# A residual kept in DRAM as one tensor per slice, with the short sequence's feed-forward layers gathering into it, and a new order of seven products

## The chip, the core and the metric

The kernel runs on one core of a Trainium2 chip. The metric is the device time of one execution in microseconds; three executions of the kernel before are known, and one more was recorded by the hardware profiler.

## What is computed

One encoder layer is applied to two sequences that share all weights: a short one, P (512 tokens), and a long one, S (1024 tokens), with 1024 channels each. All of it is fp32.

```
x = x + 1/2 * g1 * SwiGLU1(mod(RMSNorm(x)))
u = mod(RMSNorm(x)); [q|k|v|hv|hx1|hx2] = u @ w_in
a = 2-D neighbourhood attention(q, k, v)
h = bidirectional order-2 Hyena(hv, hx1, hx2)
x = x + g2 * (concat(RMSNorm(a), RMSNorm(h)) @ w_out)
x = x + 1/2 * g3 * SwiGLU2(mod(RMSNorm(x)))
...
def swiglu(x, w_gate, w_up, w_down):
    return (jax.nn.silu(x @ w_gate) * (x @ w_up)) @ w_down
```

The shifts, scales and gains (sh, sc, g1 to g3) come from a small product with `w_ada`. The hidden width of the two feed-forward layers (FFN) is 2816, that is 22 blocks of 128.

## The kernel before

**Layout.** Activations are held transposed: 128 channels on the partitions, 512 tokens along a row. A sequence's residual x is `q.xT[c]`, where c is a chunk of 512 tokens (P has one chunk, S two), and has KT = 8 slices of 128x512 in it. An fp32 product is made of three matmuls of halves (a high part and a low part of each factor), so the matmul that counts is one of 128x512, which starts about every 0.23 us when nothing stands in its way.

**The FFNs.** The 22 blocks are taken two at a time, in 11 groups g. In each group the gate and up products are formed (tiles `gu`, and `mx` in S), SiLU and product follow on ScalarE and VectorE (tiles `s`, `a`, `act`), and the down product goes slice by slice (dt = 0 to 7) into one of two PSUM banks `dn`, six matmuls each. What becomes of `dn` differs. For P (`ffn`) the residual lies in SBUF, and VectorE adds gain times `dn` to it in one instruction (`stt`, seen as `xTp<-dn` or `xRp<-dn`). For S (`ffn_fast`) the residual lies in DRAM (`q.xscr`): ScalarE writes gain times `dn` into one of four small tiles (two `s`, two `a`), and GpSimd issues a DMA that adds the tile to DRAM (line 805). Only the last group of S reads the residual back and ends as P does. S's gate and up products take seven products where eight would be usual, over sums of blocks (Strassen's way); `PRODUCTS` is the order of the seven, A and S being blocks of weights, B and T blocks of activations. B11 and B21 come from chunk 0 alone, and every T needs both chunks.

**Stages.** P's chain is narrow and S's work fills it up. `merge` takes steps of a main generator and of a side one, and the numbers in `PLAN` (cost of the main work, cost of the side work, lead of the side work, fraction) say how far the side is to be at each point of the main one. In stage A the main work is P's first FFN, and beside it stand the hyena filters of both sequences and the products with `w_ada` (DMAs into `wada6a` and `wada6b`). In stage D the main work is P's output projection and second FFN, and beside it stands S's hyena and attention. S's own FFNs run alone. By the trace stage A lies from 34 to 592 us, S's first FFN from 794 to 1487, the P projection of D from 1864 to 1930, S's hyena from 1930 to 2230, S's attention from 2230 to 2442, the tail of D to 2496, S's output projection to 2597 and S's second FFN to 3271.

**Queues.** Each engine works its instructions in program order. Weights are loaded by SyncE's queue (line 152). GpSimd issues all other DMAs (`dmb`, line 155, and the gathers, line 805) one after the other, and a DMA whose data is not there yet stops those behind it. Line 130 is the matmul; lines 116 and 118 are the instructions of VectorE and ScalarE, 118 for those of a side generator.

Of the kernel before, what the change touches and what calls it, by code (L numbers as in the profile page):

```python
# [17 lines left out]
P = 128  # L18
# [74 lines left out]
def build(ctx, tc, nc, A):  # L93
# [107 lines left out]
    for qn, L in SEQ_LEN.items():  # L201
# [20 lines left out]
        q.xscr = dp.tile([q.C, P, KT * 512], F32, name=f"xscr_{qn}")  # L222
# [285 lines left out]
    def spill_x(q):  # L508
        for c in range(q.C):
            for i in range(0, KT, 2):  # L510
                dmb(q.xscr[c][:, i * 512:(i + 2) * 512], q.xT[c][:, i:i + 2].rearrange("p k t -> p (k t)"))

    def reload_x(q, c, b):
        if c == 0:
            q.xT = []
        q.xT.append(blk(b, [P, KT, 512], F32, f"xR{q.n}"))
        dmb(q.xT[c].rearrange("p k t -> p (k t)"), q.xscr[c])


    def ffn(q, hn, wg, wu, wd, k, after, gate=None, last=None, get_dn=None,  # L520
            begin=None):
# [5 lines left out]
        def down(g, cs_, acts):  # L527
            wds = [load_unit(wd[(g * F + f) * P:(g * F + f + 1) * P, :], ()) for f in range(F)]
            for c in cs_:
                sq = SumSq()  # L530
                for dt in range(KT):
                    ps = (get_dn or dn)()
                    for f in range(F):
                        wh, wl = (wds[f][dt // 4][:, i, (dt % 4) * P:(dt % 4 + 1) * P] for i in range(2))
                        act = acts[f, c]
                        mm(ps, wh, act[:, 0:512], f == 0, False)
                        mm(ps, wh, act[:, 512:1024], False, False)
                        mm(ps, wl, act[:, 0:512], False, f == F - 1)
                    xv = q.xT[c][:, dt]
                    stt(xv, ps, q.Gc[:, k, dt:dt + 1], xv, ALU.mult, ALU.add)  # L540
                    if g == NG - 1:
                        if last is not None:
                            last.add(c, dt)
                        else:
                            sq.add(xv)
                    if dt == 3 and q.C == 1:
                        yield
                if g == NG - 1:
                    if last is not None:
                        last.done(c)  # L550
                    else:
                        after(c, sq)
                yield
        late = None
        for n, (g, cs_) in enumerate(passes):
            acts = {}
            for f in range(F):
# [33 lines left out]
                if late is not None and (f == F - 1 or n < len(passes) - 1):  # L591
                    yield from late
                    late = None
            late = down(g, cs_, acts)
# [11 lines left out]
    PRODUCTS = (("A11", "B11"), ("S1", "T1"), ("S2", "T2"), ("A12", "B21"), ("S3", "T3"), ("S4", "B22"),  # L606
# [63 lines left out]
    class Pair:  # L670
# [33 lines left out]
        def product(self, n, T):  # L704
# [3 lines left out]
            to, start = ((0, True), (2, True), (0, False), (1, True), (0, False), (2, False), (0, False))[n]  # L708
# [9 lines left out]
            elif n == 1:  # L718
                se.copy(k[3], b[2])
            elif n == 2:  # L720
                se.copy(k[1], b[0])
            elif n == 3:
                tt(k[0], k[0], b[1], ALU.add)
# [6 lines left out]
    def ffn_fast(q, fast, wg, wu, wd, k, after, last, scratch, xblocks):  # L730
# [4 lines left out]
        for g in range(NG):  # L735
# [12 lines left out]
            for n, (_, b) in enumerate(PRODUCTS):  # L748
# [3 lines left out]
                if end and n < 2:  # L752
                    if n == 0:
                        q.xT = []
                    reload_x(q, n, xblocks[n])
# [28 lines left out]
            for c in (1, 0):  # L784
                sq = SumSq()
                for dt in range(KT):
# [7 lines left out]
                    gain = q.Gc[:, k, dt:dt + 1]  # L794
                    if end:
                        xv = q.xT[c][:, dt]
                        stt(xv, ps, gain, xv, ALU.mult, ALU.add)
# [4 lines left out]
                    else:  # L802
                        y = (t_s, t_a)[dt % 2]()
                        se.activation(y, ps, AF.Copy, scale=gain)
                        nc.gpsimd.dma_start(q.xscr[c][:, dt * 512:(dt + 1) * 512], y, accum_op=ALU.add)  # L805
# [683 lines left out]
    for kt in range(KT):  # L1489
        tt(xr[kt], Pq.xT[0][:, kt], rs0, ALU.mult)  # L1490
    next(cols, None)
# [30 lines left out]
    def p_front():  # L1522
# [5 lines left out]
        yield from ffn(Pq, hn1, A["ffn1_w_gate"], A["ffn1_w_up"], A["ffn1_w_down"], 0, after, gate1, begin=begin1)  # L1528
# [15 lines left out]
    def s_input():  # L1544
# [4 lines left out]
        for c in range(2):  # L1549
# [14 lines left out]
            for kt in range(KT):  # L1564
                dmb(S.xscr[c][:, kt * 512:(kt + 1) * 512], z[c][kt])
            rows.append(rstd_rows(rstd_cols(ss, D), mx))
            yield
        fast.append(Fast(S, 0, z, rows, {"B11": 0, "T1": 5, "T2": 4, "B21": 1, "T3": 2, "B22": 3, "T4": 6}))
        for nm in ("B11", "T1", "T2", "B21"):
# [9 lines left out]
    def after1(c, sq):  # L1579
        hn2[c] = hn_pair(*((2, 3), (4, 1))[c], "hn2")  # L1580
        norm_mod(S, 1, hn2, c, sq)
    run(ffn_fast(S, fast[0], A["ffn1_w_gate"], A["ffn1_w_up"], A["ffn1_w_down"], 0, after1, None, 7, (0, 5)))
# [21 lines left out]
    def p_mixer():  # L1604
# [10 lines left out]
        w = blk(5, [P, 4096], F32, "hyP")  # L1615
# [6 lines left out]
        reload_x(Pq, 0, 5)  # L1622
# [6 lines left out]
    def after2(c, sq):  # L1629
        hn3p.append(hn_pair(2, 3, "hn3p"))  # L1630
        norm_mod(Pq, 2, hn3p, 0, sq)

    def p_back():
        yield from out_proj(Pq, mxP[0], 0, after2)
        yield from ffn(Pq, hn3p, A["ffn2_w_gate"], A["ffn2_w_up"], A["ffn2_w_down"], 2, None, None,
# [5 lines left out]
    def s_mixer():  # L1641
        fm = blk(4, [P, 4096], F32, "hyF")
        at = blk(1, [P, 4096], F32, "hyA")
# [7 lines left out]
        kT = [blk(i, [P, 4, 1024], F32R, "kTs") for i in (4, 1)]  # L1651
# [12 lines left out]
        mxS.append(hn_pair(4, 1, "mxs"))  # L1664
# [9 lines left out]
    def after3(c, sq):  # L1674
        rows3.append(rstd_of(sq.done(), D))
        z3.append([S.xT[c][:, kt] for kt in range(KT)])
        for i in range(0, KT, 2):
            dmb(S.xscr[c][:, i * 512:(i + 2) * 512], S.xT[c][:, i:i + 2].rearrange("p k t -> p (k t)"))
        if c == 0:
            fast.append(Fast(S, 2, z3, rows3, {"B11": 0, "T1": 1, "T2": 4, "B21": 6, "T3": 2, "B22": 3, "T4": 5}))  # L1680
# [8 lines left out]
    reload_x(S, 1, 5)  # L1689
# [4 lines left out]
    def any_ps():  # L1694
# [3 lines left out]
                 Final(S, any_ps, lambda c, b: t_act()), 7, (0, 1)))  # L1698
# [3 lines left out]
PLAN = {"A": (726e3, 509e3, 0.0, 0.94), "C": (321e3, 176e3, 0.0, 0.94), "D": (586e3, 413e3, 0.0, 0.94)}  # L1702
# [41 lines left out]
```

## Time and profile before

| | |
|---|---|
| median of 3 executions | 3304.14 us (3303.08 to 3305.0) |
| profiled execution, its own time | 3315.62 us |
| span of the profiled execution | 3313.8 us |
| TensorE busy (PE) | 3116.6 us, 94% |
| VectorE (DVE) | 2012.5 us, 61% |
| ScalarE (ACT) | 1440.1 us, 43% |
| GpSimd (POOL) | 548.7 us, 17% |

The time is the span and 1.8 us around it. The profiled execution took 11.5 us (0.35%) more than the median. PE is TensorE's matmuls and PEld its weight loads, which overlap them; a busy share is an average over stages that have different limits. Where busy time is shown by stretch, the columns are the stretch, its length, the busy time (and number of instructions) of PE, PEld, DVE, ACT and POOL, the granted clock of TensorE, the busy share of the 16 DMA engines, and GB/s. A row of waits gives the waiting engine, tile and line, what it waited for, the total in us, the number of times and the longest.

### The profile page before, as it was taken

What the parts mean: (1) busy time and instruction counts of PE and PEld (TensorE: products, weight loads), DVE (VectorE), ACT (ScalarE), POOL (GpSimd) and SP (SyncE); (2) the same over time, 40 slices, a digit from 0 to 9 for tenths busy, and PEclk for the clock granted to TensorE, in tenths of its full rate; (3) what the DMA queues carried; (4) which work ended last, traced back from release to release, by engine and by line L of the source; (5) the groups of instructions that cost most, each with busy time, mean ns of one, the idle gap of its engine ahead of it and who ended that gap; (6) DMA issues with size and microseconds to landing.
All of it is one profiled execution on the core that took longest, in us unless ns stands there. A gap on an engine that the chain in (4) does not pass through costs nothing. (4 is left out here: it accounts for less than half of the span.)

```text
span 3313.8 us, 41364 instructions
## 1 busy us (share of the span) xinstructions
PE 3116.6 (94%) x15283; PEld 2512.2 (76%) x15283; DVE 2012.5 (61%) x3720; ACT 1440.1 (43%) x2606; POOL 548.7 (17%) x809
## 2 busy tenths in 40 slices
PE   6989998989999999999999999989989899999998
PEld 4876777777777777777788878867768677777877
DVE  4763588768434434455676589986677734434435
ACT  3221223346444444544533332226664554544545
POOL 1121000220221221122211100002300021121120
PEclk8999999999999999999999999999989999999999
DMA  7458534464675575575335533344535375575573
GB/s 247 115 152 301 183 101 130 128 199 144 110 126 115 108 129 113 112 187 167 123 115 166 168 126 122 115 142 122 141 106 154 89 130 111 112 126 112 114 127 121
DMA packets 317690, 456.44 MB, mean 138 GB/s; under 512 B 19616, under 2 KB 224568, under 8 KB 310864
## 3 DMA queue, kind: packets, MB, share of 16 engines
q0 software_dynamic: 83600, 227.28, 30.6%
q1 hardware_dynamic: 233856, 226.52, 22.6%
q8 instruction: 120, 1.97, 0.3%
q14 instruction: 82, 0.67, 0.1%
q10 hardware_dynamic: 32, 0.01, 0.0%
HBM read 310.33 MB, written 152.78 MB: 140 GB/s over the span
## 5 line engine op out<-in xcount | busy, mean ns | idle before, releaser
L130 PE MATMUL dn<-act,hl 128*128 128x512 f32 x3168 | 775.9, 398 | 37.1 <-ACT a L116 16.2
L130 PEld LDWEIGHTS dn<-act,hl 128*128 128x128 f32 x3168 | 584.6, 189 | 209.0 <-ACT a L116 35.9
L116 DVE TENSOR_TENSOR hl<-raw,hl 128x512 fp32r<-128x512 f32 x606 | 412.5, 688 | 361.8 <-ACT hl L116 359.2
L116 ACT ACTIVATE hl<-raw 128x512 fp32r<-128x512 f32 x606 | 379.2, 630 | 563.5 <-PE gu L130 272.5
L116 DVE TENSOR_TENSOR hl<-mscA,hl 128x512 fp32r<-128x512 f32 x132 | 90.8, 689 | 342.3 <-ACT hl L116 341.1
L805 POOL DMA_DIRECT2D xscr_s<-s x160 | 136.8, 855 | 872.8 <-ACT s L116 866.3
L130 PE MATMUL gu<-hn3ph,hl 128*128 128x512 f32 x704 | 227.4, 401 | 12.0 <-DVE hl L116 9.8
L130 PE MATMUL gu<-T,hl 128*128 128x512 f32 x924 | 225.3, 391 | 5.1 <-ACT T L116 2.8
L130 PE MATMUL gu<-hn1ph,hl 128*128 128x512 f32 x704 | 226.4, 401 | 0.5 <-DVE hl L116 0.5
L130 PE MATMUL mx<-T,hl 128*128 128x512 f32 x924 | 224.2, 390 | 0.0
L130 PE MATMUL gu<-hn2h,hl 128*128 128x512 f32 x640 | 207.8, 402 | 1.8 <-DVE hl L116 1.5
L130 PEld LDWEIGHTS gu<-T,hl 128*128 128x128 f32 x924 | 172.8, 188 | 43.6 <-ACT T L116 4.3
L130 PEld LDWEIGHTS mx<-T,hl 128*128 128x128 f32 x924 | 173.3, 188 | 36.6 <-ACT act L116 0.4
L130 PEld LDWEIGHTS gu<-hn3ph,hl 128*128 128x128 f32 x704 | 134.4, 192 | 43.6 <-DVE hl L116 10.2
L130 PEld LDWEIGHTS gu<-hn1ph,hl 128*128 128x128 f32 x704 | 134.3, 193 | 40.1 <-issue 5.4
L130 PE MATMUL gu<-B,hl 128*128 128x512 f32 x660 | 160.7, 391 | 1.2 <-DVE hl L116 1.2
L130 PE MATMUL mx<-B,hl 128*128 128x512 f32 x660 | 159.9, 391 | 1.8 <-ACT act L116 1.8
L116 ACT ACTIVATE s<-dn,Gc_s 128x512 f32<-128x512 f32 x160 | 109.9, 687 | 117.2 <-DMA xscr_s<-s 82.3
L116 ACT ACTIVATE a<-dn,Gc_s 128x512 f32<-128x512 f32 x160 | 110.1, 688 | 116.7 <-DMA xscr_s<-a 82.1
L805 POOL DMA_DIRECT2D xscr_s<-a x160 | 137.0, 856 | 112.6 <-ACT a L116 107.4
L130 PEld LDWEIGHTS mx<-B,hl 128*128 128x128 f32 x660 | 124.0, 188 | 28.3 <-ACT act L116 2.2
L130 PEld LDWEIGHTS gu<-B,hl 128*128 128x128 f32 x660 | 124.2, 188 | 27.5 <-DVE hl L116 1.7
(448 smaller groups left out, 5571.6 us busy)
## 6 DMA issues: line engine op xcount, KB each, us to landing
raw<-in_ffn_w_gate SPq DMA_DIRECT2D x88, 512.0 KB, 3.9
xscr_s<-s POOLq DMA_DIRECT2D x160, 256.0 KB, 5.5
xscr_s<-a POOLq DMA_DIRECT2D x160, 256.0 KB, 5.4
raw<-in_ffn_w_up SPq DMA_DIRECT2D x66, 512.0 KB, 4.0
raw<-in_w_in SPq DMA_DIRECT2D x48, 512.0 KB, 4.3
raw<-in_ffn_w_down SPq DMA_DIRECT2D x44, 512.0 KB, 3.6
mscA<-in_ffn_w_down SPq DMA_DIRECT2D x44, 512.0 KB, 3.6
wada6a<-in_w_ada SPq DMA_DIRECT2D x12, 1024.0 KB, 7.5
```

Of the source, the lines that this page charges most:

```text
L116: return fn(*a, **k)
L130: nc.tensor.matmul(out, lhsT, rhs, start=start, stop=stop, skip_group_check=resume)
L805: nc.gpsimd.dma_start(q.xscr[c][:, dt * 512:(dt + 1) * 512], y, accum_op=ALU.add)
```

## The change

It has four parts. First, `q.xscr`, one DRAM tensor of 128x4096 per chunk, becomes eight tensors of 128x512, so that a spill or a reload of a chunk is eight DMAs of 256 KB in place of four of 512 KB or one of 2 MB. Second, P's two FFNs do as S's do: for the first ten groups ScalarE scales and GpSimd gathers, through the new function `gather`; P's residual is spilled ahead of each FFN and read back, slice by slice, after the down product of group 9. Third, `PRODUCTS` has A12 B21 in second place, and the banks and copies of `product` follow. Fourth, numbers: blocks 1 and 5 change places in several stages, and in `PLAN` the costs of the main work of A and D fall by 53e3 and the side work of A gets a lead of 0.08.

```diff
-        q.xscr = dp.tile([q.C, P, KT * 512], F32, name=f"xscr_{qn}")
+        q.xscr = [[dp.tile([P, 512], F32, name=f"xscr{c}{k}_{qn}") for k in range(KT)] for c in range(q.C)]
...
-    def spill_x(q):
-        for c in range(q.C):
-            for i in range(0, KT, 2):
-                dmb(q.xscr[c][:, i * 512:(i + 2) * 512], q.xT[c][:, i:i + 2].rearrange("p k t -> p (k t)"))
+    def spill_x(q, cs=None):
+        for c in range(q.C) if cs is None else cs:
+            for k in range(KT):
+                dmb(q.xscr[c][k], q.xT[c][:, k])
...
         q.xT.append(blk(b, [P, KT, 512], F32, f"xR{q.n}"))
-        dmb(q.xT[c].rearrange("p k t -> p (k t)"), q.xscr[c])
...
+        for k in range(KT):
+            dmb(q.xT[c][:, k], q.xscr[c][k])
+
+    def gather(q, k, c, dt, ps):
+
+        y = (t_s, t_a)[dt % 2]()
+        se.activation(y, ps, AF.Copy, scale=q.Gc[:, k, dt:dt + 1])
+        nc.gpsimd.dma_start(q.xscr[c][dt], y, accum_op=ALU.add)
...
-                    xv = q.xT[c][:, dt]
-                    stt(xv, ps, q.Gc[:, k, dt:dt + 1], xv, ALU.mult, ALU.add)
                     if g == NG - 1:
+                        xv = q.xT[c][:, dt]
+                        stt(xv, ps, q.Gc[:, k, dt:dt + 1], xv, ALU.mult, ALU.add)
                         if last is not None:
                             last.add(c, dt)
                         else:
                             sq.add(xv)
+                    else:
+                        gather(q, k, c, dt, ps)
...
                     late = None
+                    if g == NG - 1:
+                        reload_x(q, 0, xblock)
...
-    PRODUCTS = (("A11", "B11"), ("S1", "T1"), ("S2", "T2"), ("A12", "B21"), ("S3", "T3"), ("S4", "B22"),
+    PRODUCTS = (("A11", "B11"), ("A12", "B21"), ("S1", "T1"), ("S2", "T2"), ("S3", "T3"), ("S4", "B22"),
                 ("A22", "T4"))
...
-                if end and n < 2:
-                    if n == 0:
-                        q.xT = []
-                    reload_x(q, n, xblocks[n])
+                if end and n in (0, 2):
+                    reload_x(q, n // 2, xblocks[n // 2])
...
-PLAN = {"A": (726e3, 509e3, 0.0, 0.94), "C": (321e3, 176e3, 0.0, 0.94), "D": (586e3, 413e3, 0.0, 0.94)}
+PLAN = {"A": (673e3, 509e3, 0.08, 0.94), "C": (321e3, 176e3, 0.0, 0.94), "D": (533e3, 413e3, 0.0, 0.94)}
```

Three places of the program show what moves. The first is VectorE in S's hyena, late in stage D; `hyA` and `hyz` are the hyena's tiles, `hl` the halves of P's weights, `xRp` P's residual. Before:

```order
L116 TENSOR_TENSOR hl<-raw,hl 128x512
L116 SCALAR_TENSOR_TENSOR xRp_14116<-dn,Gc_p,xRp_14116 128x512 x2
L116 TENSOR_TENSOR hl<-raw,hl 128x512
L118 TENSOR_TENSOR hyA_14153<-hyA_14153,mx 128x512
L116 TENSOR_TENSOR hl<-raw,hl 128x512
L118 TENSOR_TENSOR hyA_14153<-hyA_14153,mx 128x512 x3
L116 SCALAR_TENSOR_TENSOR xRp_14116<-dn,Gc_p,xRp_14116 128x512
L118 TENSOR_TENSOR hyA_14153<-hyA_14153 128x2x256
L116 SCALAR_TENSOR_TENSOR xRp_14116<-dn,Gc_p,xRp_14116 128x512
```

With the change, at the same point of the hyena:

```order
L116 TENSOR_TENSOR hl<-raw,hl 128x512
L118 TENSOR_TENSOR hyz6b<-mx,hyz6b 128x512 x2
L118 TENSOR_TENSOR hyA_14385<-hyA_14385,mx 128x512 x4
L118 TENSOR_TENSOR hyA_14385<-hyA_14385 128x2x128
L118 TENSOR_TENSOR hyA_14385<-hyA_14385 128x2x256
L116 TENSOR_TENSOR hl<-raw,hl 128x512
L118 TENSOR_TENSOR hyA_14385<-hyA_14385 128x2x256
```

The additions to P's residual are gone from VectorE's queue; nothing takes their place there.

The second is GpSimd in S's attention, where `atS<-gwin` are loads of the bias, `mscA<-qscr_s` and `mscA<-vwin_s` loads of queries and values. Before:

```order
L155 DMA atS_16600<-gwin 16x1024 x2
L155 DMA mscA<-qscr_s 128x2x128
L155 DMA atS_16600<-gwin 16x1024
L155 DMA mscA<-vwin_s 128x3x256
L155 DMA atS_16600<-gwin 16x1024
L155 DMA atS_16600<-gwin 64x1024
```

With the change:

```order
L155 DMA atS_16889<-gwin 16x1024 x2
L155 DMA mscA<-qscr_s 128x2x128
L155 DMA atS_16889<-gwin 16x1024
L155 DMA mscA<-vwin_s 128x3x256
L155 DMA atS_16889<-gwin 16x1024
L155 DMA atS_16889<-gwin 64x1024
L524 DMA xscr_p<-s 128x512
L524 DMA xscr_p<-a 128x512
L524 DMA xscr_p<-s 128x512
L524 DMA xscr_p<-a 128x512
L155 DMA mscA<-qscr_s 128x2x128 x2
L155 DMA mscA<-vwin_s 128x3x256
```

The gathers (line 524 of the changed kernel) stand between the loads of one step of the attention and those of the next.

The third is GpSimd at the end of stage D, after the attention's last load, up to the spill that follows S's output projection. Before, nothing of P is there:

```order
L155 DMA mscA<-vwin_s 128x3x256
L155 DMA xRs_18958<-xscr_s 128x4096
L155 DMA xRs_19337<-xscr_s 128x4096
L155 DMA xscr_s<-xRs_18958 128x1024 x4
L155 DMA xscr_s<-xRs_19337 128x1024 x4
```

With the change, the gathers of group 9 and the reloads of P's residual (`xRp<-xscr_p`) alternate:

```order
L155 DMA xRs_19390<-xscr_s 128x512 x8
L524 DMA xscr_p<-s 128x512 x2
L155 DMA xRp_19399<-xscr_p 128x512
L524 DMA xscr_p<-a 128x512 x2
L155 DMA xRp_19399<-xscr_p 128x512
L524 DMA xscr_p<-s 128x512
L155 DMA xRp_19399<-xscr_p 128x512
L524 DMA xscr_p<-a 128x512
L524 DMA xscr_p<-s 128x512
L155 DMA xRp_19399<-xscr_p 128x512
L524 DMA xscr_p<-a 128x512
L155 DMA xRp_19399<-xscr_p 128x512 x4
```

Eight gathers and eight reloads have come in; a reload waits for the landing of the gather of its slice, and the gathers behind it wait with it. The same stands at the end of stage A.

## Rows read from the trace of the kernel before

**Rows 1.** The page: span, and busy time of TensorE and of VectorE

```profile
span 3313.8 us, 41364 instructions
...
PE 3116.6 (94%) x15283; PEld 2512.2 (76%) x15283; DVE 2012.5 (61%) x3720; ACT 1440.1 (43%) x2606; POOL 548.7 (17%) x809
```

**Rows 2.** Busy time by stretch: A, hyena, attention, S's second FFN

```profile
34.00:592.00 558.00, 516.18 (x2725) 402.49 (x2724) 359.57 (x645) 144.05 (x252) 53.00 (x92) 0.96 0.52 165
...
1930.00:2230.00 300.00, 285.07 (x1452) 241.02 (x1452) 278.64 (x489) 85.59 (x140) 17.16 (x32) 0.97 0.40 123
2230.00:2442.00 212.00, 201.41 (x1196) 154.40 (x1196) 139.79 (x409) 134.04 (x300) 59.05 (x93) 0.98 0.46 137
...
2597.00:3271.00 674.00, 650.31 (x2793) 520.88 (x2794) 310.09 (x470) 333.53 (x547) 136.89 (x162) 1.00 0.61 117
```

**Rows 3.** Waits of TensorE, 1930 to 2230: total, times, longest (us)

```profile
PE gu L130 <- DVE hl L116: 9.8, 1, 9.8
PE mx L130 <- DVE hyA L118: 3.4, 3, 1.5
```

**Rows 4.** VectorE's groups, 2060 to 2195: busy us, mean ns, idle before

```profile
L116 DVE SCALAR_TENSOR_TENSOR xRp<-dn,Gc_p,xRp 128x512 f32<-128x512 f32 x29 | 21.5, 748 | 0.1
...
L118 DVE TENSOR_TENSOR hyA<-hyA,mx 128x512 f32<-128x512 f32 x16 | 10.8, 683 | 3.3 <-PE mx L130 3.0
```

**Rows 5.** Waits of TensorE in stage A, 34 to 592

```profile
PE mx L130 <- DVE r L118: 10.4, 12, 1.8
PE mx L130 <- DMA wada6b<-in_w_ada: 8.8, 4, 6.6
```

**Rows 6.** VectorE's additions to P's residual, stage A

```profile
L116 DVE SCALAR_TENSOR_TENSOR xTp<-dn,Gc_p,xTp 128x512 f32<-128x512 f32 x88 | 65.4, 747 | 16.4 <-PE dn L130 16.2
```

**Rows 7.** Busy time by stretch, the first 66 us of stage A

```profile
34.00:100.00 66.00, 58.96 (x318) 41.31 (x318) 34.28 (x78) 20.94 (x38) 1.08 (x2) 0.84 0.63 203
```

**Rows 8.** Waits of TensorE at the start of S's second FFN, 2597 to 2660

```profile
PE gu L130 <- DVE hl L116: 3.6, 2, 2.4
PE gu L130 <- ACT T L116: 2.8, 2, 2.5
```

**Rows 9.** Groups of TensorE, ScalarE and GpSimd, S's second FFN, 2597 to 3271

```profile
L130 PE MATMUL dn<-act,hl 128*128 128x512 f32 x969 | 235.9, 398 | 17.7 <-ACT a L116 8.8 <-ACT s L116 5.8 <-ACT hl L116 2.4
...
L116 ACT ACTIVATE a<-dn,Gc_s 128x512 f32<-128x512 f32 x80 | 55.0, 688 | 58.9 <-DMA xscr_s<-a 42.3 <-PE dn L130 16.0
...
L155 POOL DMA_DIRECT2D xRs<-xscr_s x2 | 1.1, 554 | 7.9 <-DVE hl L116 5.0 <-PE mx L130 2.9
```

**Rows 10.** The page's DMA issues: KB each, median us from issue to landing

```profile
xscr_s<-s POOLq DMA_DIRECT2D x160, 256.0 KB, 5.5
```

**Rows 11.** The page's groups: GpSimd's issue of a gather

```profile
L805 POOL DMA_DIRECT2D xscr_s<-s x160 | 136.8, 855 | 872.8 <-ACT s L116 866.3
```

**Rows 12.** DMA, 794 to 1487: a queue's packets, MB, share; a read of 256 KB

```profile
q0 software_dynamic: 25464, 51.65, 45.6%
...
mscB<-hscr_p POOLq DMA_DIRECT2D x2, 256.0 KB, 4.9
```

**Rows 13.** DMA, 220 to 400: a queue's packets, MB, share of 16 engines

```profile
q1 hardware_dynamic: 21273, 37.81, 62.8%
q0 software_dynamic: 2551, 8.08, 13.7%
```

**Rows 14.** VectorE's additions to P's residual, 220 to 400: shortest, median, longest (ns)

```profile
L116 DVE SCALAR_TENSOR_TENSOR xTp<-dn,Gc_p,xTp x32: 742/750/752, 256.3 to 399.8; 128x512 f32<-128x512 f32 x32
```

**Rows 15.** The end of stage D in order of time: start and length (us)

```profile
2458.78 23.89 PE L130 MATMUL dn<-act,hl 128*128 128x512 f32 x96
...
2482.74 0.75 DVE L116 SCALAR_TENSOR_TENSOR xRp<-dn,Gc_p,xRp 128x512 f32<-128x512 f32 x1
```

**Rows 16.** GpSimd's waits in S's attention, 2230 to 2442

```profile
POOL mscA L155 <- DVE mscA L118: 94.2, 24, 12.1
...
POOL atS L155 <- DVE st L118: 22.0, 9, 5.7
```

## The prediction on record

> **What bounds the kernel now.** I read the page first: TensorE works 3116.6 of 3313.8 us, VectorE 2012.5 [rows 1]. That is 94%, so no change off TensorE can give more than the 197 us that TensorE stands still, and only where it stands still for what the change touches. So I went to the stretches. In S's second FFN TensorE has 650.31 of 674 us, in stage A 516.18 of 558, in S's hyena 285.07 of 300, in S's attention 201.41 of 212 [rows 2]. The reader is to see that the hyena is the one stretch in which another engine is as full as TensorE: VectorE has 278.64 of 300 us there, against 359.57 of 558 in A. Then I read, for each of these, what ended TensorE's waits, and last the rows of the things that the change adds: the gather's ScalarE copy, its issue, its landing, and the share of the DMA engines.
>
> **The change part by part.**
>
> *VectorE's additions leave P's FFNs.* Of the 88 additions in a stage [rows 6] the 80 of groups 0 to 9 go, 0.747 us each, 60 us of VectorE in A and as much in D. In the hyena TensorE waited once 9.8 us for the low halves of weights and 3.4 us in three waits for `hyA` [rows 3]. The long one is a backlog: from 2060 to 2195 VectorE made 29 additions, 21.5 us, and in that stretch its large groups show 3.3 us of idle time [rows 4]. It was late by 9.8 us after 135 us of unbroken work, and 21.5 us of that work goes; so this wait should go whole. From below it is nothing (if the splitting of weights waits for ScalarE instead), from above both waits, 13.2. I take 12.
>
> In A VectorE is 64% busy. TensorE's waits for it are 12 of at most 1.8 us for `r`, 10.4 in all [rows 5], each the end of a short chain in a filter; an addition of 0.75 us stands ahead of some of them. Bounds 0 and 10.4; I take 4, nearer to the lower one because a chain's own latency stays.
>
> *The order of the seven products.* At the start of S's second FFN TensorE waits 2.8 us for the first T and 3.6 us for halves of weights [rows 8], 6.4 together. Now two products of chunk 0 (A11 B11 and A12 B21) stand ahead of the first T where there was one. A product for gate and up is 24 matmuls, at 0.243 us (235.9 over 969 [rows 9]) 5.8 us: more than the wait for T. I take 5, bounds 0 and 6.4. In S's first FFN the blocks are made long before, and I count nothing; in the steady groups the same matmuls stand in another order, and I count nothing: the products of a pair are as long as before, and each bank is read by the same copy.
>
> *The lead of 0.08 in A.* Side work stands ahead in the first 66 us, where TensorE loses 7 us (58.96 of 66) at a granted clock of 0.84 [rows 7]. It can fill what is empty, or push P's first group back by as much: 7 either way. I take a gain of 3, because the stretch is idle for P's own chain.
>
> *P's gathers by themselves.* A gather is a ScalarE copy of 0.69 us [rows 9], an issue of 0.86 [rows 11] and 5.5 us from issue to landing [rows 10]: a tile is used again after 7.05 us at best, and with four tiles one gather can go every 1.76 us, while six matmuls of 0.243 give a slice every 1.46. In S this costs TensorE 8.8 and 5.8 us per 160 gathers [rows 9], in runs of 16. P's runs are of 8 at most: the first four have free tiles, the other four fall behind by 4 times 0.3 us, 1.2, less than the one spare bank covers (1.46). ScalarE has room (144.05 of 558 us in A [rows 2], and 55 more). I take a loss of 2, bounds 0 and 14.6.
>
> *The reload at the end of A and of D.* Before, the last two down products of D ran without a break, 96 matmuls in 23.89 us, 1.49 a slice, and the last addition began at 23.96 and ended at 24.7 [rows 15]. Now I follow GpSimd's queue as it stands, from the start of the down product. Gathers 0 and 1 are issued at 2.2 and 3.7 and land at 7.7 and 9.2. Reload 0 waits for 7.7; gathers 2 and 3 behind it go at 8.2 and 9.1 and land at 13.7 and 14.6; reload 1 at 9.9, gather 4 at 10.5, landing at 16.0; reload 2 waits for 13.7; gather 5 goes at 14.3. Gather 6 needs gather 2's tile, copied from 13.7 to 14.4, and goes at 15.1; reload 3 at 16.0 (0.55 us an issue [rows 9]); gather 7 (tile of gather 3, copied until 15.3) goes at 16.5 and lands at 22.0; then reload 7, which takes about 4.9 us [rows 12], to 26.9. TensorE gets the bank of slice 6 at 14.4 in place of 11.9, ends slice 7 of group 10 at 26.3, and the last addition runs from 26.9 to 27.7: 3.0 us later than before. Nothing hides it, since what follows is the norm of this very residual. Twice 3 is 6; bounds 0 and 12 (three landings stand in the chain, and another 1 us on each gives 3 more at either place).
>
> *DMA traffic.* In S's first FFN GpSimd's queue takes 45.6% of 693 us, 316 us for 51.65 MB [rows 12]; a gather's 0.262 MB are 1.6 us of all 16 engines, 2.0 if the whole share is put on the 160 gathers. From 220 to 400 us the `w_ada` loads run, SyncE's queue has 62.8%, GpSimd's 13.7% [rows 13], 42 us are free, and 32 additions fall there [rows 14] which become 51 to 64 us of gathers: 9 to 22 us too many. TensorE already waits 8.8 us there for `wada6b` [rows 5]. That speaks for a loss of up to 22. Against it: a gather need not land at once (nothing but its tile waits for it), and the loads of 280 to 400 can move into what follows. I take 3. The Trainium skill's page "DMA: Bandwidth & Descriptors", section "Issuing engines are not separate DMA queues", says that DMAs of all issuing engines run on the same 16 engines and interleave; by that rule alone the queues' shares add, and the sum would take the 9 us for the 3 and come out at a loss of 4 us for the kernel in place of a gain of 10. No row of this kernel shows both kinds of traffic above 100% at once.
>
> The prologue's new spill is 2.1 MB, by the rate above 13 us of all engines if it delays the first weights one for one; in the first 66 us of A the DMA share is 0.63 [rows 7], which leaves 24 us. I take 1, bounds 0 and 13. Spills and reloads in smaller pieces move the same bytes; the eight issues cost 4.4 us of a GpSimd that waits most of the time, hidden as the one was.
>
> *GpSimd in S's attention.* Its queue is busy 59.05 of 212 us [rows 2] and waits 94.2 and 22.0 for VectorE [rows 16]; those waits are loads that stand ready early. In the new order 26 gathers stand between the first load of queries and the last of values, singly and in runs of up to four, 0.855 us each, 22 in all; a load behind a run of four is up to 3.4 us later. I take 2, bounds 0 and 22.
>
> **Sum.** Gains 12 + 4 + 5 + 3 = 24; losses 2 + 6 + 3 + 1 + 2 = 14; net 10 us less. The profiled execution would go from 3315.6 to 3305.6; it stands 0.35% above the median, and the same 10 us off the median of 3304.1 give **3294 us**. A measurement of this kernel tells about 0.2%, 6.6 us, from no change, so the forecast is faster, not by much.
>
> **The rivals.**
>
> *It cancels (3298 to 3311, say 3303).* The hyena's wait shrinks to what ScalarE and the matmuls' own chain allow, 5 in place of 12, and A gives 1: then 14 of gain stand against 14 of loss. For it: TensorE is at 95% in the hyena [rows 2], and in-order engines pass a delay on. Against it: 21.5 us of backlog go where 9.8 were missed.
>
> *Slower through GpSimd's queue in the attention.* If each run of gathers holds the loads behind it back with no slack, the attention loses the 22 us, and the kernel takes 3294 - 2 + 22 = 3314. It decides against the change from 12 us on (the 10 of the sum and its own 2), 0.46 us for each gather, more than half of its issue. For it: loads of queries and values stand right behind the gathers in the new order. Against it: GpSimd's long waits show that loads stand ready before their data.
>
> *Slower through DMA traffic at the `w_ada` loads.* All 22 us lost there: 3294 - 3 + 22 = 3313. It decides from 13 us on.
>
> *One tensor per slice frees S's FFNs.* If S's gathers waited for each other because they add to one tensor, the split would take away the 14.6 us of each S FFN, twice: 3294 - 29 = 3265. Against it: ScalarE's 42.3 us of waiting there [rows 9] is for a tile of the gather four before, which the split leaves as it is.
>
> **Numbers.** Forecast 0.48, cancelling 0.26, attention 0.12, DMA 0.09, freed FFNs 0.05. Faster is 0.53 (the first and the last), same 0.26, slower 0.21. The range runs from 3270 (the bounds of the gains, 13.2 + 10.4 + 6.4 + 7 = 37, with a few losses) to 3316 (either slow rival with the bounds of the reload). The forecast's own range is 3284 to 3298.
>
> **What would show it.** In the changed profile: the 9.8 us wait of `gu` for `hl` in the hyena gone, and VectorE near 245 of some 290 us there; the T wait after S's output projection gone; in the tails of A and D some 3 us more between the last down products and the norm; TensorE's waits for `wada6a` and `wada6b` grown by a few us and not by ten; the attention no longer than before by more than 2 or 3 us; and S's FFNs at the same pace, with waits of `dn` for ScalarE as before. Wrong would be a new wait of TensorE in the attention, or `w_ada` waits above 20 us.

## The result, and the profile after

The changed kernel takes 3363.9 us (median of four executions, 3358.67 to 3369.39); the kernel before took 3304.57 on the same chip (3303.08 to 3311.54). The ratio is 1.0176 [1.0153, 1.0198]: 59 us slower, where 10 us less were forecast. All ratios below are to the kernel before, run on the same chip in the same job, and 0.1% is 3.3 us.

First the page of the profiled execution (3365.27 us): the span, the busy time of the engines, and two of the DMA issues (KB each, median us from issue to landing).

```profile
span 3363.1 us, 41952 instructions
...
PE 3142.4 (93%) x15283; PEld 2522.6 (75%) x15283; DVE 1910.2 (57%) x3560; ACT 1544.0 (46%) x2769; POOL 749.9 (22%) x1070
...
xscr_s<-s POOLq DMA_DIRECT2D x160, 256.0 KB, 5.2
...
xscr_p<-s POOLq DMA_DIRECT2D x80, 256.0 KB, 6.1
```

VectorE lost 102 us of work against [rows 1], and the kernel is slower all the same. TensorE does the same 15283 matmuls in 26 us more busy time, at a mean granted clock of 0.968 for 0.976. Next the busy time by stretch, in the columns of [rows 2] and for the same four: A, S's hyena, S's attention, S's second FFN.

```profile
36.00:643.00 607.00, 533.90 (x2723) 411.57 (x2724) 317.89 (x585) 198.49 (x337) 131.50 (x187) 0.92 0.70 191
...
1974.00:2265.00 291.00, 278.18 (x1419) 234.13 (x1419) 247.62 (x440) 113.77 (x186) 59.66 (x81) 0.98 0.66 171
2265.00:2496.00 231.00, 215.54 (x1231) 164.70 (x1232) 126.48 (x390) 152.84 (x331) 85.18 (x124) 0.96 0.64 158
2653.00:3320.00 667.00, 650.79 (x2789) 519.56 (x2788) 308.43 (x468) 333.16 (x546) 146.24 (x176) 0.99 0.61 118
```

Most of the loss is in A: 607 us for 558. Of these 49 us, 31 are idle time of TensorE (607 - 533.9 = 73.1, before 558 - 516.18 = 41.8), and 18 are longer busy time for the same matmuls at a mean clock of 0.92 in place of 0.96. The waits of TensorE there (total, times, longest), beside [rows 5]:

```profile
PE mx L130 <- DVE r L118: 18.8, 11, 5.3
PE mx L130 <- DMA wada6b<-in_w_ada: 16.1, 6, 4.5
PE mx L130 <- DMA wada6a<-in_w_ada: 13.5, 6, 4.2
...
PE dn L130 <- ACT s L116: 4.8, 2, 3.0
...
PE dn L130 <- ACT a L116: 2.9, 2, 2.2
```

The wait for `r` was to become shorter, and is 18.8 for 10.4. `wada6a` was 3.5 in all before, and 13.5 now.

Now stage D. The hyena is counted from P's first gate product to the attention's first product with keys, the attention from there to its last one, the tail from there to the first transposition of P's result. Before and after, the hyena went from 302.9 to 290.8 us, the attention from 197.3 to 215.5, the tail from 57.3 to 65.8. P's matmuls for gate and up stand in other places now (34 of them, 7.7 us at 0.227, later than the attention's first product; 14 more than before within the attention and 20 in the tail). Without that shift the hyena gained 4.4 us, the attention lost 15.0 and the tail 4.0: stage D is 14.6 us longer (15.0 + 4.0 - 4.4). S's first FFN took 690.5 for 693.3, its second 667 for 674.

### The profile page after: what moved, and what is told of

Read it like the earlier page. It is cut to its first block, busy times and chain, and to the rows that moved or that the text cites. A ratio compares the mean times of both kernels' runs of the same rounds, so it can differ in the third digit from the quotient of the medians.

```text
span 3363.1 us, 41952 instructions
## 1 busy us (share of the span) xinstructions
PE 3142.4 (93%) x15283; PEld 2522.6 (75%) x15283; DVE 1910.2 (57%) x3560; ACT 1544.0 (46%) x2769; POOL 749.9 (22%) x1070
## 5 line engine op out<-in xcount | busy, mean ns | idle before, releaser
L130 PE MATMUL dn<-act,hl 128*128 128x512 f32 x3168 | 786.9, 401 | 43.4 <-ACT a L116 19.9
```

Of the source, the lines that this page charges most:

```text
L130: nc.tensor.matmul(out, lhsT, rhs, start=start, stop=stop, skip_group_check=resume)
```

## The experiments

They are told by question and not in the order of their numbers. The n-th matmul is TensorE's n-th of the whole execution, told by its start in the profiled one. In e1, e2, e7, e8, e12 and e14 `ffn` has a parameter `ngath`, the number of groups that gather, set for A and D apart; the other kernels are the change with the one edit shown.

**e1_vector_adds.** P's additions go back to VectorE in A and in D, P's spills go, `PLAN` is that of before; the slices, the new order of products and the places of the blocks stay.

```diff
-                    if g == NG - 1:
+                    if g < ngath:
+                        gather(q, k, c, dt, ps)
+                    else:
                         xv = q.xT[c][:, dt]
                         stt(xv, ps, q.Gc[:, k, dt:dt + 1], xv, ALU.mult, ALU.add)
...
-PLAN = {"A": (673e3, 509e3, 0.08, 0.94), "C": (321e3, 176e3, 0.0, 0.94), "D": (533e3, 413e3, 0.0, 0.94)}
+PLAN = {"A": (726e3, 509e3, 0.0, 0.94), "C": (321e3, 176e3, 0.0, 0.94), "D": (586e3, 413e3, 0.0, 0.94)}
```

> The change without P's gathers: VectorE adds to P's residual in both FFNs again, and PLAN has its old numbers; the tensors per slice, the order of the products and the blocks stay changed. If P's gathers (with what they do to the order in stage A and to GpSimd's queue) carry the whole loss, this run stands at or below the kernel before: 3296 to 3306. If the smaller DMAs or the order of the products carry some of it, it stands above 3311.

Measured: 0.9955 [0.9941, 0.9969], the lowest ratio of all runs. Slices, order and blocks together gain 15 us; the whole loss, and more, comes with P's gathers, their spills and reloads, and their numbers in `PLAN`.

**e2_gather_d_only.** As e1, with `ngath` 10 in D (and D's number and spill as in the change).

> P gathers in stage D alone; in stage A VectorE adds, with the old numbers of A. By the two traces stage D pays 22 us in the attention and 2 in the tail and gains 12 in the hyena, so this run should stand 10 to 14 us above the run without P's gathers, about 3312, and the other 50 us of the change belong to stage A. If D's parts do not add up that way (the attention's loss comes from what A left behind, or the hyena's gain is from elsewhere), it stands within 3 us of the run without gathers or more than 25 above.

Measured: 1.0001 [0.9988, 1.0013]. So the gathers of D lose 15 us against e1, and those of A, with spill, number and lead, 58 us against e2. That these two less the 15 us that e1 gains make up the whole is no test, since each is a difference of neighbours. A test is the trace: stage D is 14.6 us longer in the changed kernel too.

**e8_slices_alone.** The kernel before with one tensor per slice and nothing else (old order of products, old blocks).

> The kernel before with the residual as one tensor per slice (spills and reloads of 256 KB) and nothing else. The run without P's gathers gained 0.45%, 5 us of it in S's first FFN, 3.5 in the stage after it, 6 in S's second FFN. If the new order of the products carries this, the slices alone change nothing: ratio 0.999 to 1.001. If the smaller reloads and spills carry it: ratio 0.995 to 0.997.

Measured: 0.9964 [0.9953, 0.9975], 12 us. It overlaps e1's interval: what the order of the seven products is worth by itself isn't resolved. Here is TensorE's group of down products in S's second FFN (matmuls, busy us, mean ns; idle time before them), beside [rows 9], and this kernel's page, beside [rows 10].

```profile
L130 PE MATMUL dn<-act,hl 128*128 128x512 f32 x973 | 235.4, 396 | 13.1 <-ACT s L116 8.3 <-ACT a L116 3.3 <-ACT hl L116 0.8
```

```profile
xscr_s<-s POOLq DMA_DIRECT2D x160, 256.0 KB, 5.3
xscr_s<-a POOLq DMA_DIRECT2D x160, 256.0 KB, 5.3
```

The wait is 13.1 for 17.7, with landings of 5.3 us for 5.5 (`s`) and 5.4 (`a`). In the profiled executions S's first FFN gives back 3.4 us, the stretch from its end to the second FFN 3.9, and the second FFN 5.3; the waits of the down products show 4.6 of the last and 2.4 (16.6 to 14.2) of the first. What shortens the rest stays open; the run has smaller spills and reloads too.

**e7_hyena_gather and e12_four_groups.** As e1, but D gathers in its first six or four groups, which lie beside the hyena, then reads P's residual back and lets VectorE add, so that nothing of it stands in the attention or the tail. D's number in `PLAN` is 554e3 with six groups and 565e3 with four.

```diff
-                    if g == NG - 1:
+                    if g == ngath and ngath > 0:
                         reload_x(q, 0, xblock)
...
-        yield from ffn(Pq, hn3p, A["ffn2_w_gate"], A["ffn2_w_up"], A["ffn2_w_down"], 2, None, 1, None,
+        yield from ffn(Pq, hn3p, A["ffn2_w_gate"], A["ffn2_w_up"], A["ffn2_w_down"], 2, None, 1, 6, None,
```

> P gathers in stage D for groups 0 to 5 alone, those that fall beside S's hyena; then the residual is read back and VectorE adds for the rest; stage A has no gathers. If the hyena's gain (12.6 us between the runs with and without D's gathers) and the loss in attention and tail (20.6 and 8.5) come each from the gathers in that stretch, the loss goes and the gain stays: ratio 0.990 to 0.993. If the reload at the start of the attention costs as much as the gathers did: ratio 0.996 to 1.000.

> P gathers in stage D for groups 0 to 3 alone, with the reload ending inside S's hyena, away from the attention's first loads; no gathers in A. Some 14 of the 29 additions of the unbroken stretch of VectorE are gone, 10 us, as much as TensorE's long wait of 9.8 us. If that wait goes and nothing takes its place: ratio 0.991 to 0.994. If the reload or the order of the hyena takes it back as with six groups: 0.995 to 0.999.

Measured: 0.9966 [0.9948, 0.9983] with six and 0.9975 [0.9958, 0.9992] with four. Neither beats e1. TensorE's longest waits in the hyena, of e1, of six groups and of four:

```profile
PE gu L130 <- DVE hl L116: 9.8, 1, 9.8
```

```profile
PE mx L130 <- DVE hyA L118: 8.7, 4, 3.5
PE mx L130 <- DMA mscA<-vwin_s: 7.6, 1, 7.6
```

```profile
PE mx L130 <- DVE hyA L118: 11.3, 5, 4.7
```

The wait of 9.8 us for the weights' halves is gone in both, as forecast, and others have grown: all waits listed for the stretch sum to 25.3 us with six groups and 16.5 with four, and to 20.0 in e1. So none of the 9.8 shows as a gain, even where the attention and the tail are kept clear. The 12.6 us that e7's expectation took from two traces were a gain of 4.9 at most: 34 matmuls of P (7.7 us at 0.227) stand in the hyena of e1 and behind it in e2.

**e3_no_lead.** The change with a lead of 0.0 for A's side work.

> The change with the lead of the side work in stage A back at 0.0 and nothing else. Theory 'bunching': the loss of A comes from the w_ada products standing back to back on TensorE with no matmuls of P's FFN between them, as the new order has it from 256 to 313 us; with no lead the order has FFN matmuls between them again, so most of the 50 us of stage A go: 3315 to 3330. Rival 'queue': P's gathers stand in GpSimd's queue behind the 34 DMAs of the bias table, which are there without the lead as well: the time stays at 3350 to 3365. Rival 'traffic': gathers and w_ada loads share the DMA engines; the same bytes move, so 3350 to 3365 too.

Measured: 1.0179 [1.0152, 1.0207], as the change itself. That the lead bunches the `w_ada` products is seen in the trace (below), but without it the loss is the same.

**e4_table_late.** The change, with the bias table, whose DMAs stand in GpSimd's queue from 234 to 274 us, built after S's filters.

```diff
...
-                                lambda: filters(S, 7, *mixed_msc()), s_input))
+                                lambda: filters(S, 7, *mixed_msc()), late_table, s_input))
```

> The change with the bias table (34 DMAs of GpSimd) built after S's filters in place of just before the w_ada products; the lead stays 0.08. Rival 'queue': the gathers of P's group at 256 us are issued at once and most of the 50 us of stage A go: 3315 to 3330. Theory 'bunching': six w_ada products still stand back to back in this order, half as many in a row as in the change's; a part of the loss stays: 3330 to 3350. Rival 'traffic': the same bytes move, 3350 to 3365.

Measured: 1.0206 [1.0183, 1.0229], no faster than the change. That the table is the cause had rested on this stretch of GpSimd's timeline in the changed kernel (start, us, idle before and its releaser):

```profile
234.02 3.62 POOL L155 DMA_DIRECT2D gscr<-rpb  x6 [2.83 <-DVE rpb L118]
...
266.23 0.55 POOL L155 DMA_DIRECT2D gwin<-gscr  x1 [6.64 <-DMA gscr<-rpb]
...
273.71 1.20 POOL L155 DMA_DIRECT2D gscr<-rpb  x2
274.90 1.00 POOL L524 DMA_DIRECT2D xscr_p<-s  x1
```

The gather at 274.90 had its data since 258.35 (ScalarE's copy, 0.67 us from 257.68), and stood behind the table for 16.6 us. In e4 this hold-up is gone, and the 2800th matmul starts at 612.4 us in place of 624.4. But S's first FFN begins at 863.4 in place of 846.0 (behind 3882 matmuls and 3861): at its new place, 733 to 773 us, the table stands ahead of S's input (`zx`), and TensorE's waits for that are 16.8 us from 600 to 870 in place of 2.4. So the table among the gathers costs some 12 us in A, by one trace of each, and its new place costs more; the run doesn't clear the table.

**e6_filter_loads_sync and e11_queue_cleared.** e6 is the change with the filters' loads of `decay`, `hy_wo` and `hy_skip` issued by SyncE (the last is shown, the others alike); e11 has that, the late table and no lead.

```diff
-                dmb(skl, A["hy_skip"][o:o + 1, cb * P:(cb + 1) * P].partition_broadcast(P))
+                dma(skl, A["hy_skip"][o:o + 1, cb * P:(cb + 1) * P].partition_broadcast(P))
```

> The change with the filters' small loads (decay, hy_wo, hy_skip) issued by SyncE's queue in place of GpSimd's; the gathers and all bytes stay. Theory 'queue': a filter's loads no longer stand behind gathers that wait for ScalarE, so the filters of P (100 to 220 us) run at the old pace and 10 to 20 us go: ratio 1.011 to 1.015. Theory 'traffic': nothing changes, ratio 1.016 to 1.019; above that if SyncE's weight loads now stand behind the filters' loads.

> The change with full gathers, no lead, the filters' loads issued by SyncE and the bias table built after S's filters: what stood between the gathers in GpSimd's queue up to the w_ada loads is away, but the bytes stay. Theory 'queue': 1.002 to 1.009. Rival 'traffic': 1.013 to 1.018.

Measured: 1.0164 [1.0146, 1.0182] and 1.0264 [1.0232, 1.0296]. In e6 P's second group of down products starts at 154.6 us in place of 163.6, and the thousandth matmul at 211.8 in place of 221.4, so the loads behind gathers do hold the filters back. At the 2800th 5 of these 10 us are left, and S's first FFN begins at 847.1 for 846.0. Now SyncE's queue waits for the filters, 76.5 us from 95 to 345 in e6, 85.0 in e11, where it was 13.9 in the change:

```profile
SPq L152 <- DVE fT6b L118: 76.5, 12, 11.1
```

TensorE's waits for `wada6b` and `wada6a` are 32.0 in e6 for 29.6. Clearing one in-order queue into another moves the wait. In e11 the table's late place weighs more: TensorE waits 34.6 us for `zx`. So e11 speaks for neither theory.

**e9_copies_alone, e13_copies_no_lead.** The change with A's gathers left out behind ScalarE's copy; e13 without the lead too.

```diff
+        if q.C == 1 and k == 0:
+            return
         nc.gpsimd.dma_start(q.xscr[c][dt], y, accum_op=ALU.add)
```

> The change with P's gathers of the first FFN left out behind ScalarE's copy (nothing is added to P's residual there): no issue by GpSimd, no bytes. The lead and its order stay, with the w_ada products back to back. The run with an eighth of the bytes gave 1.0113, the change 1.0176, the run with D's gathers alone 1.0001. Theory 'GpSimd's queue has the rest': with the DMAs gone stage A is as before, ratio 0.999 to 1.004. Rival 'the order has the rest' (the w_ada products in a row, ScalarE's copies): ratio 1.007 to 1.013.

> As the run with copies alone (P's first-FFN gathers left out behind ScalarE's copy), but with no lead in stage A. With the lead that run stood at 1.0063, 0.6% above the run with VectorE's additions in A. Theory 'the lead and its bunched order cost this': without the lead ratio 0.998 to 1.002. Rival 'ScalarE's copies and the order that comes with them cost it': 1.004 to 1.008.

Measured: 1.0063 [1.0043, 1.0082] and 1.0041 [1.0021, 1.0062]. Of the 58 us between e2 and the change, A's gathers cost 37 us with the lead (e9 to the change); without it they cost 46 (e13 to e3). In e13 the first down product of P starts at 97.7 us, in e2 at 92.1; TensorE waits 13.8 and 8.6 us there for the first weights (`raw`, from 0 to 100 us). The spill of P ahead of A stands in e13 and not in e2. But the change has it too, waits 4.5 us for `raw`, and starts that product at 92.5, so the price of the spill isn't shown.

**e5_small_gathers, e10_small_no_lead.** The change with gathers in A that add 64 of the 512 columns, so that the issues stay and an eighth of the bytes; e10 without the lead.

```diff
-        nc.gpsimd.dma_start(q.xscr[c][dt], y, accum_op=ALU.add)
+        w = 64 if q.C == 1 and k == 0 else 512
+        nc.gpsimd.dma_start(q.xscr[c][dt][:, 0:w], y[:, 0:w], accum_op=ALU.add)
```

> The change with P's gathers of the first FFN cut to an eighth: ScalarE's copy and GpSimd's issue are all there, but each DMA adds 64 of the 512 columns (the other columns are left out of P's residual). Theory 'queue': the 50 us of stage A are lost because gathers and the filters' DMAs wait for each other in GpSimd's one queue; they still do, so the time stays within 15 us of the change's: ratio to the kernel before 1.013 to 1.018. Theory 'traffic': the gathers' bytes crowd the w_ada and weight loads; seven eighths of them are gone, so 30 us or more of the 50 go: ratio 1.003 to 1.009.

> The change with an eighth of the bytes in P's first-FFN gathers (the other columns left out) and no lead in stage A. Traffic and the bunched order are both away, the issues in GpSimd's queue stay. Theory 'queue': 1.009 to 1.013, as with the small gathers and the lead. Rival 'traffic and order': 0.999 to 1.005.

Measured: 1.0113 [1.0093, 1.0134] and 1.0085 [1.0056, 1.0113]. Both lie below what queue alone was to give and above what traffic alone was to leave: the bytes have a price, and the issues have one.

**e14_lead_alone.** e1 with the lead of 0.08.

> The run without P's gathers (0.9955) with a lead of 0.08 in stage A and nothing else. Theory 'the lead costs by itself': six w_ada products stand nearly in a row, ratio 0.999 to 1.003. Rival 'the lead costs nothing while VectorE adds': 0.994 to 0.997. A lead that gains, as the prediction took it (3 us): 0.993 to 0.995.

Measured: 0.9989 [0.9976, 1.0001]. Where it stands alone, the lead costs 11 us.

A's loss step by step, from e2 on (the intervals of neighbours in a row are apart, but for e13 and e10, which overlap a little; between the rows those of e9 and e13, and of e5 and e10, overlap, so the lead's part isn't resolved there):

| | gathers nowhere in A | copies, spill, reload, A's number 673e3 | and 80 small DMAs | and all bytes |
|---|---|---|---|---|
| no lead | 1.0001 (e2) | 1.0041 (e13) | 1.0085 (e10) | 1.0179 (e3) |
| lead 0.08 | | 1.0063 (e9) | 1.0113 (e5) | 1.0176 (the change) |
| the step, us | | 13 (21 with the lead) | 15 to 17 | 21 to 31 |

This table shows where in A the two steps with the lead come up, in the profiled executions:

| start of matmul, us | thousandth | 1500th | 2800th |
|---|---|---|---|
| e9, no DMAs | 210.8 | 336.6 | 587.5 |
| e5, small DMAs | 211.9 | 347.9 | 598.7 |
| the change, all bytes | 221.4 | 368.4 | 624.4 |

The issues cost nothing clear beside P's filters (1 us by the thousandth matmul) and 10 from there to the 1500th, where the bias table and 149 of the 192 `w_ada` matmuls stand. None of those stands ahead of the thousandth. The bytes cost 10 us beside the filters, 11 more there and 5 behind. Without the lead the bytes' 33 us are spread alike (9, 15 and 9 in e3 against e10); where the issues' come up isn't resolved (1 us at the 1500th, 4 at the 2800th).

Here is the stretch from 220 to 340 us, where the `w_ada` loads run, in e2, e5 and the change (columns as in the stretches above, then packets, MB and share of SyncE's queue, q1, and of GpSimd's, q0).

```profile
220.00:340.00 120.00, 107.34 (x527) 71.43 (x526) 47.55 (x84) 23.56 (x41) 21.05 (x36) 0.96 0.84 282
...
q1 hardware_dynamic: 12900, 27.95, 68.8%
q0 software_dynamic: 2177, 5.82, 15.1%
```

```profile
220.00:340.00 120.00, 92.85 (x411) 55.82 (x413) 24.18 (x44) 27.62 (x45) 34.58 (x52) 0.83 0.84 269
...
q1 hardware_dynamic: 10448, 24.64, 60.2%
q0 software_dynamic: 4573, 7.64, 23.1%
```

```profile
220.00:340.00 120.00, 85.97 (x373) 48.88 (x372) 24.48 (x47) 24.38 (x40) 35.81 (x55) 0.77 0.94 293
...
q1 hardware_dynamic: 8968, 23.44, 54.9%
q0 software_dynamic: 4493, 11.65, 38.9%
```

GpSimd's share goes up by 24 points from e2 to the change and the weights' share goes down by 14; together they reach 94%. But 9 of the 14 are gone in e5 already, at 83% together, and fewer matmuls want fewer weights: from e5 to the change GpSimd gains 16 points and the weights lose 5. A gather there lands after 7.3 to 7.6 us (median), in e5 a small one after 4.0 to 5.2; the loads of `wada6a` land after 7.1 us, where e2 has 7.5 (those of `wada6b` after 6.3 and 6.0):

```profile
wada6a<-in_w_ada SPq DMA_DIRECT2D x9, 1024.0 KB, 7.1
```

```profile
wada6a<-in_w_ada SPq DMA_DIRECT2D x10, 1024.0 KB, 7.5
```

## Why the prediction was wrong

The step that failed is the one by which the losses of A's gathers were taken near their lower bounds: "a gather need not land at once (nothing but its tile waits for it)". The sum had 2 us for P's gathers by themselves, in both stages, and 3 for their traffic. In A alone they cost 37 to 46 us (e9 to the change, e13 to e3). What waits for the tile is P's next slice. ScalarE's waits in stage A for a tile that a gather still holds, in the change and in e5, which differs by the bytes alone:

```profile
ACT s L116 <- DMA xscr_p<-s: 17.8, 8, 3.8
ACT a L116 <- DMA xscr_p<-a: 14.4, 10, 3.4
```

```profile
ACT s L116 <- DMA xscr_p<-s: 1.5, 1, 1.5
ACT a L116 <- DMA xscr_p<-a: 1.0, 1, 1.0
```

That is 32.2 us for 2.5, and without the lead 25.1 (e3) for 4.1 (e10). The prediction's own working gives as much for a later landing: with 7.5 us, as from 220 to 340, in place of 5.5 four tiles let a gather go every 2.26 us, and four slices fall behind by 3.2 us in each of ten groups, more than the spare bank's 1.46. That these waits are how the bytes cost 21 to 31 us is argued: they grow by 30 and 21 us, the runs by 21 and 31, and no run has more tiles.

Behind a gather the queue waits too, and the forecast looked at GpSimd's queue in the attention and at the tails and had no term for it in A. A gather stands there ahead of the loads and stores of the filters and of the bias table, and behind them. From 100 to 345 us the changed kernel's GpSimd waits 111 us for ScalarE's copies, with the filters' DMAs behind it, and 58 us for the filters, with the gathers behind it:

```profile
POOL xscr_p L524 <- ACT s L116: 66.4, 10, 44.0
POOL kscr_p L155 <- DVE fT6b L118: 58.1, 5, 20.0
POOL xscr_p L524 <- ACT a L116: 44.9, 8, 26.6
```

These rows alone show no loss: in the kernel before, GpSimd waits 127.0 us for the filters in the same stretch. That the queue ties streams together is shown by the 10 us by which e6 is ahead at the thousandth matmul, and by the gather that stands 16.6 us behind the table. What e10, e5, e9 and e13 show is the price, 15 to 17 us for 80 issues with an eighth of the bytes. Those bytes are in that price, so it is an upper bound for the queue alone. Term by term:

- *Hyena, gain 12.* The mechanism was right: the 9.8 us wait is gone and VectorE is busy 247.6 of 291 us ("near 245 of some 290"). The gain was 4.4. The waits of [rows 3] sum to 13.2; what now stands there is 4.7 for `hyA`, 3.0 and 1.4 for ScalarE's copies of `dn`. As in e7 and e12, the backlog had covered waits of the chain behind it.
- *A's VectorE relief, gain 4.* It did not come: the `r` waits grew by 8.4. They are not shorter without gathers either: 15.6 us from 34 to 643 in e13, 11.7 in e2.
- *Order of products, gain 5.* Of the 6.4 us in [rows 8], 2.4 (`hl`) and 1.8 (`T`) stay, so 2.2 are gained. The wait for T went down and not away.
- *Lead, gain 3.* It costs 11 us with VectorE's additions (e1 to e14); with the copies the ratios differ by 7 us, which isn't resolved, and with the whole change nothing shows.
- *P's gathers by themselves, 2; spill, 1; reload in A, 3.* Copies, spill and reload without any gather cost 13 in A, with A's number of 673e3 in it, and 21 with the lead; this isn't split further. The gathers themselves are told above.
- *Reload in D, 3.* It is 7.0 by the chain from the start of the last down product to the norm: 34.4 us (2510.08 to 2544.51) for 27.4 (2458.78 to 2486.21).

```profile
2510.08 5.56 PE L130 MATMUL dn<-act,hl 128*128 128x512 f32 x18
2514.02 0.89 POOL L524 DMA_DIRECT2D xscr_p<-s  x1 [23.05 <-ACT s L116]
...
2524.49 0.69 ACT L116 ACTIVATE a<-dn,Gc_p 128x512 f32<-128x512 f32 x1 [4.25 <-DMA xscr_p<-a]
2525.23 11.55 PE L130 MATMUL dn<-act,hl 128*128 128x512 f32 x42 [3.00 <-ACT a L116]
...
2540.70 0.75 DVE L116 SCALAR_TENSOR_TENSOR xRp<-dn,Gc_p,xRp 128x512 f32<-128x512 f32 x1
2544.51 1.87 PE L130 MATMUL gu<-ones,r 128*128 128x1 f32 x8 [3.88 <-DVE r L116]
```

  The queue went as the prediction followed it; the first gather was issued 3.9 us after the start, not 2.2, landings took 6.0 (median) and not 5.5, and the last addition stands at 30.6 for the 26.9 forecast. Of these 7.0 the tail as a whole shows 4.0; ahead of the down products, and without the shifted matmuls, it is 3.1 shorter.
- *DMA traffic at the `w_ada` loads, 3.* The bytes cost 21 to 31 us in all of A, about as much as the upper bound of 22 or more, but only 11 to 15 of them come up between the thousandth and the 1500th matmul. The waits for `wada6b` and `wada6a` grew by 17 us, and the stretch was called wrong "above 20": they stand at 29.6. But they stand at 19.8 in e9, which has the lead and no gather in A. The rule weighed there, in the Trainium skill's page "DMA: Bandwidth & Descriptors", section "Issuing engines are not separate DMA queues", agrees with this trace as far as it goes: both queues' traffic runs on the same engines in the same stretch (54.9% and 38.9%). That the `w_ada` loads lost by it isn't shown, since they land hardly later (7.1 us for 7.5 with `wada6a`, 6.3 for 6.0 with `wada6b`); the gathers do. The prediction also added wrongly there: with 9 us in place of 3 its sum is 24 less 20, a gain of 4 and not "a loss of 4 us".
- *GpSimd in the attention, 2.* It is 15. ScalarE's wait for queries went from 11.3 to 20.8 us (first row of before, then of the change, over the same stage), and TensorE's wait for ScalarE's `mscA` is five times and 8.9 us in all, where it was once and 4.6. The loads of queries land later, 4.0 us for 3.0 (medians over the same stage), with the DMA engines busy for 0.64 of the time and not 0.46:

```profile
ACT mscA L118 <- DMA mscA<-qscr_s: 11.3, 10, 2.6
...
mscA<-qscr_s POOLq DMA_DIRECT2D x31, 128.0 KB, 3.0
```

```profile
ACT mscA L118 <- DMA mscA<-qscr_s: 20.8, 11, 3.6
...
mscA<-qscr_s POOLq DMA_DIRECT2D x31, 128.0 KB, 4.0
```

  So the issues in GpSimd's queue, which the term priced, and the traffic are not told apart here. No run tests the one without the other.

The rivals named two of the places. They were priced as if one of them would come alone, 3313 or 3314; together, by the prediction's own prices, they give 3333 (3294 with 22 and 22 in place of 2 and 3). They lie in different stages and came together, with A's queue and tiles on top. The fourth rival, slices that free S's FFNs, came true in part: 9 us of the 29 in the two FFNs (3.4 and 5.3), and the argument against it had left out that a landing itself could become shorter.

## What to carry to other kernels

An accumulating DMA in place of a VectorE addition isn't free because VectorE was full: ask what else stands in the issuing engine's queue at that moment, and whether the DMA engines have room in that very stretch. Here it lost beside the filters, the `w_ada` loads and the attention; that it pays for S's FFNs, which have it in both kernels and run alone, no run tests. And ask what waits for its landing: here ScalarE waited 32 us for four small tiles when the landings were 2 us later than forecast. Losses in different stages are terms and no alternatives: several small risks taken at their lower ends sum to a wrong sign. And a part of a change that looks like a mere layout, one tensor per slice, may be the only one that is worth keeping: it gives 0.9964 of the time before, and 0.9955 with the new order.

## What the runs showed of the hardware that was not expected

Adding to a tensor of its own per slice, rather than to a slice of a larger one, lands in 5.2 or 5.3 us (`xscr_s<-s`, median, in all fifteen traces with that layout) and not 5.5 (the one trace of the kernel before), with the same tiles, bytes and issues. The rows of such a tensor stand 2 KB apart in DRAM in place of 16 KB; which of the two does it no run tells.

Waits for loads were followed by the lower clock. In the changed kernel the `w_ada` products stand nearly back to back from 256 us on, and the granted clock is at its lower level (1.2 of 2.4 GHz) from 259.1 to 279.5 us, from within a wait of 3.81 us on; the same eight matmuls take 1.07 us at first and 1.93 after waits of 3.81 and 2.64 us:

```profile
255.38 1.07 PE L130 MATMUL mx<-wada6a,cs 128*32 128x512 f32 x8
...
260.92 1.93 PE L130 MATMUL mx<-wada6b,cs 128*32 128x512 f32 x8 [3.81 <-DMA wada6b<-in_w_ada]
265.49 1.93 PE L130 MATMUL mx<-wada6a,cs 128*32 128x512 f32 x8 [2.64 <-DMA wada6a<-in_w_ada]
```

```profile
259.10:279.50 20.40, 10.60 (x40) 3.00 (x41) 1.17 (x5) 0.82 (x2) 6.14 (x10) 0.50 0.89 304
```

From 220 to 340 us the granted clock is 0.77, a mean of the two levels, where e2 has 0.96. So a wait for weights can cost a second time, in the busy time of what follows. Of A's 49 us 18 are longer busy time, and by an estimate most of it lies here: busy time times what the clock lacks of 1 is 20 us in this stretch of the change (85.97 at 0.77) and 4 in e2 (107.34 at 0.96).
